# One encoder layer on one Trainium2 core: the FFN up product with seven block products in place of eight

## Chip, core and metric

The kernel runs on one core of one Trainium2 chip. The metric is the device time of one execution in microseconds (us). A profiled execution also leaves a trace: what each engine did (PE is the matrix engine, PEld its weight loads, DVE the vector engine, ACT the scalar engine, POOL the GpSimd engine, SP the engine whose queue issues nearly all transfers here), and what it waited for.

## The reference, cut to what matters

Two batches (`x_prompt`, `x_sample`) of 512 tokens and 1024 columns go through one layer with shared weights. The change is in the last part and at the passage into it:

```python
x = x + (g_a * a_out + g_b * b_out) @ w_o          # (512, 1024), each batch
xn2 = _rmsnorm(x, norm2_g)
up = xn2 @ w_up                                    # (1024) x (1024, 6144)
gate, val = jnp.split(up, 2, axis=-1)              # 3072 columns each
gate = _dwconv(gate, ffn_conv_w, ffn_conv_b)       # 3 taps over the tokens
x = x + (jax.nn.gelu(gate) * val) @ w_down         # (3072) x (3072, 1024)
```

## The kernel before

All data are 32-bit. Every matrix product is made of three matmuls: each operand is split into a rounded part `hi` and a remainder `lo`, and hi x hi, hi x lo and lo x hi are added up in a PSUM bank. A matmul has a 128 x 128 stationary operand and 512 moving columns.

The order of instructions on each engine is the order in which the program emits them; nothing reorders them. Weights come through one list of slabs (128 x 512), `specs`, in the order of use. `Stream.adv` splits the next slab: `hi` is an ACT copy (L225), `lo` a POOL subtraction (L226). `Stream.loads` issues the slabs' transfers on SP up to three ahead, and a ring of eight `hi`/`lo` pairs holds what PE has not used yet.

The stages at the end of the kernel:

- For each batch, `mix_tile` (8 times), then `o_phase`: 16 groups of 12 matmuls (L984 to L986) into `pso`, each added to the residual tile `acc[t]` (128 tokens x 1024) by DVE (L987). All eight `acc` tiles stay in SBUF to the end.
- After a tile's last group, `norm2_tile` squares and sums it on ACT (L286), makes the factor on POOL (L287, L288) and scales the tile into a copy `x2s` on POOL (L290). `norm2_T` transposes it on PE (L967) and splits it: DVE times the gain (L970), ACT `x2h` (L971), DVE `x2l` (L972).
- `up(f)`, for 24 column tiles f: gate and value columns, both batches, 8 depth blocks, 3 matmuls, into two-bank PSUM tiles; so 96 matmuls per f (L148 to L150). `gate_conv` and `h_out` make the convolution, the GELU, the product with the value half and its split `hh`, `hl`.
- `down(f)`, for pairs of f, stands between the `up` calls (`ffn_order`): 16 groups of 6 matmuls (L1090 to L1092), each added to `acc` by DVE (L1093).

Of the kernel before, what the change touches and what calls it, by code (L numbers as in the profile page):

```python
# [19 lines left out]
D = 1024  # L20
# [43 lines left out]
class Stream:  # L64
# [6 lines left out]
    def __init__(self, specs, load, split, cap, bufs):  # L71
        self.specs, self.load, self.split, self.cap, self.bufs = specs, load, split, cap, bufs
        self.raw, self.out = {}, {}
        self.nl = self.ns = self.nu = 0
        self.live = {}

    def loads(self):
        while self.nl < min(len(self.specs), self.ns + self.cap):
            self.raw[self.nl] = self.load(self.specs[self.nl])
            self.nl += 1  # L80

    def adv(self, n):

        self.loads()
        for _ in range(n):
            if self.ns == len(self.specs):
                return
# [25 lines left out]
def layer_kernel(ctx: ExitStack, tc: tile.TileContext, xs_in, norm1_g, w_in, conv_w, conv_b, lru_wa, lru_ba,  # L113
# [21 lines left out]
    o_d = dram.tile([S, 512], F32, name="o_d")  # L135

# [56 lines left out]
    def up_specs(f):  # L193
        return col_slabs(w_up, 128 * f, KD) + col_slabs(w_up, FF + 128 * f, KD)

    def down_specs(f):
        return [row_slab(w_down, f + j, 512 * h) for j in range(2) for h in range(2)]

    ffn_order = [("u", 0)]
    for f in range(1, NF - 3, 2):  # L200
        ffn_order += [("u", f), ("u", f + 1), ("d", f - 1)]
    ffn_order += [("u", NF - 3), ("u", NF - 2), ("u", NF - 1), ("d", NF - 4), ("d", NF - 2)]
    for t, f in ffn_order:
        specs += up_specs(f) if t == "u" else down_specs(f)
# [3 lines left out]
    def wload(spec):  # L208
        r = sa.tile([128, 512], F32, tag="raw", bufs=3, name="raw")
        _, src, nk = spec  # L210
        if nk:
# [5 lines left out]
    def wsplit(spec, r):  # L217
        ring, _, nk = spec
        n = 128 * nk if nk else 512
# [6 lines left out]
        lo_eng[0].tensor_tensor(out=lo[:, 0:n], in0=r[:, 0:n], in1=hi[:, 0:n], op=ALU.subtract)  # L226
        return hi, lo

    ws = Stream(specs, wload, wsplit, 3, {"a": 8, "b": 8})
    ws.open_ring("a")  # L230

# [575 lines left out]
    def combine(t, cg):  # L807
        d = p3.tile([128, 3, 8], F32, tag="cd", bufs=2, name="cd")
        e = p3.tile([128, 3, 8], F32, tag="ce", bufs=2, name="ce")
        m = p3.tile([128, 8], F32, tag="cm", bufs=2, name="cm")  # L810
# [96 lines left out]
    cm_acc0, acp0 = open_pool("acc0")  # L907
    cm_x20, x20p = open_pool("x2T0")
    cm_m, mp = open_pool("mix")
# [3 lines left out]
    def load_acc(b, pool):  # L913
        for i in range(4):
            acc[4 * b + i] = pool.tile([128, D], F32, name=f"acc{4 * b + i}")
            SP.dma_start(out=acc[4 * b + i], in_=xs_in[b][0, 128 * i:128 * i + 128, :])

    def new_x2(b, pool):
        x2[b] = (pool.tile([128, KD, S], F32R, name=f"x2h{b}"), pool.tile([128, KD, S], F32R, name=f"x2l{b}"))
# [11 lines left out]
    def mix_tile(b, c):  # L931
# [12 lines left out]
        mh = mp.tile([128, S], F32R, tag=f"mh{c}", bufs=1, name="mh")  # L944
        ml = mp.tile([128, S], F32R, tag=f"ml{c}", bufs=1, name="ml")
# [9 lines left out]
    def norm2_tile(t):  # L955
        x_t = mp.tile([128, D], F32, tag="x2s", bufs=3, name="x2s")
# [3 lines left out]
    def norm2_T(t):  # L960
        x_t = xst.pop(t)
        h, l = x2[t // 4]
        tl = slice(128 * (t % 4), 128 * (t % 4) + 128)
        for kk in range(0, KD, 4):
            pst = ps3.tile([128, 4, 128], F32, tag="t", bufs=4, name="pst")
# [27 lines left out]
    load_acc(0, acp0)  # L993
# [3 lines left out]
    new_x2(0, x20p)  # L997
# [3 lines left out]
    def hook0(n, i):  # L1001
# [168 lines left out]
```

## Time and profile before

| | |
|---|---|
| time, median of 3 runs | 2149.46 us (2149.22 to 2152.23) |
| profiled execution, its own time | 2149.69 us |
| its span in the trace | 2147.6 us |
| PE busy | 2087.7 us, 97% |
| PEld, DVE, ACT, POOL busy | 82%, 51%, 36%, 28% |
| mean granted TensorE clock | 0.99 of 2.4 GHz |
| data moved | 182 MB, mean 85 GB/s |

A matmul's shown duration overlaps the next one's, so PE's pace is read from the starts of matmuls that follow each other, and idle time from what stands between them. The time lies some 2 us above the span: what starts and ends the execution outside of the instructions.

### The profile page before, as it was taken

Reading aid. Unit: us, or ns where it says so; the run is one execution under the profiler, and the core shown is the slowest. Engines: PE = TensorE matmul, PEld = TensorE weight load, DVE = VectorE, ACT = ScalarE, POOL = GpSimd, SP = SyncE. Lnnn points to the kernel's source line nnn. Section 1 sums busy time; section 2 is a strip of 40 time slices with the busy share of each in tenths; the row PEclk is TensorE's granted clock in tenths of the full one; section 3 lists DMA queues with packets and bytes.
Section 4 is the critical chain, followed back from the end, with each engine's and each line's share of the span. In section 5 each row is a group of like instructions: output and inputs, shape, how many; then the busy total and the mean of one; then the engine's idle time right before and its main releaser. Section 6 shows DMA issues by size and latency. Waiting matters only on the chain. (4 is left out here: it accounts for less than half of the span.)

```text
span 2147.6 us, 25951 instructions
## 1 busy us (share of the span) xinstructions
PE 2087.7 (97%) x9859; PEld 1760.8 (82%) x9859; DVE 1084.7 (51%) x1581; ACT 783.5 (36%) x1321; POOL 601.7 (28%) x538
## 2 busy tenths in 40 slices
PE   7998898999999999999999999999999999999999
PEld 5876676887899999998777888888888888888887
DVE  5599998717862671675663442432233332333324
ACT  4388888622331242135433332422212122212120
POOL 3111111025113421413346455522222212221220
PEclk9999999999999999999999999999999999999999
DMA  4434354411111111103556445211111111111112
GB/s 143 150 104 133 106 141 130 146 50 40 36 41 46 40 54 54 36 16 119 186 180 193 145 151 174 65 38 57 49 49 47 52 40 50 49 51 47 54 45 84
DMA packets 190299, 181.98 MB, mean 85 GB/s; under 512 B 27708, under 2 KB 142942, under 8 KB 190174
## 3 DMA queue, kind: packets, MB, share of 16 engines
q1 hardware_dynamic: 188126, 175.08, 26.7%
q0 software_dynamic: 2048, 5.25, 1.0%
q8 instruction: 78, 1.28, 0.2%
q14 instruction: 47, 0.39, 0.1%
HBM read 141.80 MB, written 33.23 MB: 82 GB/s over the span
## 5 line engine op out<-in xcount | busy, mean ns | idle before, releaser
L226 POOL TENSOR_TENSOR lo<-raw,hi 128x512 fp32r<-128x512 f32 (+1 forms) x332 | 427.6, 1302 | 914.5 <-ACT hi L225 870.8
L225 ACT CAST hi<-raw 128x512 fp32r<-128x512 f32 (+1 forms) x376 | 219.6, 607 | 319.5 <-issue 117.9
L148 PE MATMUL ps<-x2h,hi 128*128 128x512 f32 x768 | 299.0, 389 | 0.0
L149 PE MATMUL ps<-x2l,hi 128*128 128x512 f32 x768 | 298.9, 389 | 0.0
L150 PE MATMUL ps<-x2h,lo 128*128 128x512 f32 x768 | 298.8, 389 | 0.0
L757 PE MATMUL ps<-hi,xh 128*128 128x512 f32 x576 | 251.4, 436 | 0.0
L758 PE MATMUL ps<-lo,xh 128*128 128x512 f32 x576 | 228.5, 397 | 0.0
L759 PE MATMUL ps<-hi,xl 128*128 128x512 f32 x576 | 228.3, 396 | 0.0
L1093 DVE TENSOR_TENSOR acc<-acc,psd 128x512 f32<-128x512 f32 x192 | 131.8, 687 | 190.8 <-PE psd L1092 190.8
L148 PE MATMUL ps<-xh,hi 128*128 128x512 f32 x544 | 219.4, 403 | 4.4 <-DVE xc L353 4.4
L150 PE MATMUL ps<-xh,lo 128*128 128x512 f32 x544 | 216.8, 399 | 0.0
L149 PE MATMUL ps<-xl,hi 128*128 128x512 f32 x544 | 216.8, 399 | 0.0
L149 PEld LDWEIGHTS ps<-x2l,hi 128*128 128x128 f32 x768 | 144.2, 188 | 30.1 <-DVE x2l L972 0.3
L148 PEld LDWEIGHTS ps<-x2h,hi 128*128 128x128 f32 x768 | 144.2, 188 | 29.8
L150 PEld LDWEIGHTS ps<-x2h,lo 128*128 128x128 f32 x768 | 144.2, 188 | 29.8
L757 PEld LDWEIGHTS ps<-hi,xh 128*128 128x128 f32 x576 | 156.1, 271 | 9.6
L758 PEld LDWEIGHTS ps<-lo,xh 128*128 128x128 f32 x576 | 158.3, 275 | 5.9
L759 PEld LDWEIGHTS ps<-hi,xl 128*128 128x128 f32 x576 | 156.4, 271 | 8.0
L1090 PE MATMUL psd<-hi,hh 128*128 128x512 f32 x384 | 149.4, 389 | 0.0
L1091 PE MATMUL psd<-lo,hh 128*128 128x512 f32 x384 | 149.4, 389 | 0.0
L1092 PE MATMUL psd<-hi,hl 128*128 128x512 f32 x384 | 149.4, 389 | 0.0
L1048 DVE SCALAR_TENSOR_TENSOR gc<-ps,vff,gc 128x1022 f32<-128x1022 f32 x24 | 30.8, 1282 | 225.3 <-ACT gc L1047 225.3
(188 smaller groups left out, 3467.0 us busy)
## 6 DMA issues: line engine op xcount, KB each, us to landing
raw<-in_w_in_dram SPq DMA_DIRECT2D x144, 256.0 KB
raw<-in_w_up_dram SPq DMA_DIRECT2D x96, 256.0 KB
raw<-in_w_down_dram SPq DMA_DIRECT2D x48, 256.0 KB
sg_d<-sgt SPq DMA_DIRECT2D x16, 512.0 KB
raw<-in_w_lru_out_dram SPq DMA_DIRECT2D x32, 256.0 KB
raw<-in_w_o_dram SPq DMA_DIRECT2D x32, 256.0 KB
cg<-num_d SPq DMA_DIRECT2D x24, 264.0 KB
num_d<-num SPq DMA_DIRECT2D x23, 264.0 KB
```

The lines of the kernel that those rows point to most:

```text
L148: PE.matmul(out=ps, lhsT=a, rhs=b, start=(k == 0), stop=False)
L149: PE.matmul(out=ps, lhsT=a, rhs=rl(k), start=False, stop=False)
L150: PE.matmul(out=ps, lhsT=wl(k), rhs=b, start=False, stop=(k == n - 1))
L225: A.copy(out=hi[:, 0:n], in_=r[:, 0:n])
L226: lo_eng[0].tensor_tensor(out=lo[:, 0:n], in0=r[:, 0:n], in1=hi[:, 0:n], op=ALU.subtract)
L757: PE.matmul(out=ps, lhsT=a, rhs=hi, start=(k == 0), stop=False)
L758: PE.matmul(out=ps, lhsT=a, rhs=lo, start=False, stop=False)
L759: PE.matmul(out=ps, lhsT=b, rhs=hi, start=False, stop=(k == KD - 1))
L1090: PE.matmul(out=ps, lhsT=a[0][:, tl], rhs=w[0], start=(i == 0), stop=False)
L1091: PE.matmul(out=ps, lhsT=a[0][:, tl], rhs=w[1], start=False, stop=False)
L1092: PE.matmul(out=ps, lhsT=a[1][:, tl], rhs=w[0], start=False, stop=(i == 1))
L1093: V.tensor_tensor(out=acc[t][:, cl], in0=acc[t][:, cl], in1=ps, op=ALU.add)
```

## The change

Take the up product's operands in 2 x 2 blocks: weights by column half (gate, value) and depth half, tokens by depth half and batch. Eight block products become seven, of 12 matmuls each (four depth blocks times three): per f 84 matmuls, not 96. With A11, A12 the two depth halves of a gate slab and A21, A22 those of the value slab, DVE makes the sums S1 to S4 of weights in SBUF before they are split. The sums of tokens are T1 to T4, with B11, B21 the depth halves of batch 0 and B22 the lower one of batch 1; each is kept as `hi` and `lo`. Products A11·B11, S2·T2, S3·T3 and A22·T4 add up in one bank (`pfA`), S1·T1 and S4·B22 in another (`pfC`), A12·B21 in a third (`pfB`); the partial sums wanted in between are copied out by ACT or added by DVE.

`acc` now holds one batch: each tile goes to DRAM (`acc_d`, L970) after its last `o_group`. For batch 1 `norm2_own` scales the tile in place, and `sums_T` transposes it and makes T1 to T4 and B22 (for a tile of 128 tokens: nine DVE, five ACT and four POOL instructions). For the first three f the two products without batch 1 (`batch0`) come first, between the transposes of tiles 0 to 3; the other five (`rest`) follow. Each f's result goes to DRAM (`f_d`), and the down product comes after all 24, with new `acc` tiles read back from `acc_d`.

```diff
+    def up_split(f, nm):
+        w = lambda key: upw[f, key]
+        add = lambda out, x, y, op: V.tensor_tensor(out=out, in0=x, in1=y, op=op)
+        if nm == ("S2" if f < EARLY else "A12"):
...
+            add(w("S1"), w("A21"), w("A22"), ALU.add)
+            add(w("S2"), w("S1"), w("A11"), ALU.subtract)
+        out = split_to("a", w(nm))
+        if nm == "S2":
+            add(w("A21"), w("A11"), w("A21"), ALU.subtract)
+            upw[f, "S3"] = w("A21")
+            add(w("A12"), w("A12"), w("S2"), ALU.subtract)
+            upw[f, "S4"] = w("A12")
...
+    def norm2_own(t):
+
+        store_acc(t)
+        junk = ps3.tile([128, D], F32, tag="m", bufs=2, name="junk")
...
+        act(out=junk, in_=acc[t], func=AF.Square, accum_out=ss)
+        G.tensor_scalar(out=ss, in0=ss, scalar1=1.0 / D, scalar2=EPS, op0=ALU.mult, op1=ALU.add)
+        G.tensor_tensor(out=rs, in0=ss, in1=mhalf[:, 0:1], op=ALU.pow)
+        V.tensor_scalar(out=acc[t], in0=acc[t], scalar1=rs, scalar2=None, op0=ALU.mult)
+
+    def sums_T(i, pst):
...
+        old = lambda nm, j: x2[nm][j][:, :, tl]
+        lo22 = put("B22", b22, G)
+        tt(V, t, b12, old("B11", 0), ALU.subtract)
+        tt(V, t, t, old("B11", 1), ALU.subtract)
+        lo22()
+        lo1 = put("T1", t, V)
+        tt(G, b12, b22, b12, ALU.subtract)
+        lo3 = put("T3", b12, G)
+        lo3()
+        tt(V, b22, b22, t, ALU.subtract)
+        lo1()
+        lo2 = put("T2", b22, V)
+        tt(V, t, old("B21", 0), b22, ALU.subtract)
+        lo2()
+        tt(V, t, t, old("B21", 1), ALU.add)
+        put("T4", t, G)()
...
+    lo_eng[:] = [V, G]
+    h0, h1 = ws.take(4), None
+    for n, (i, hlf) in enumerate(((0, 0), (1, 0), (0, 1), (1, 1), (2, 0), (2, 1), (3, 0), (3, 1))):
+        if n == 2:
+            h1 = ws.take(4)
+        o_group(4 + i, 1, hlf, h1 if hlf else h0, n >= 6)
+        if n < 6:
+            ws.adv(2)
+        if hlf:
+            norm2_own(4 + i)
+        if n in (5, 7):
+            sums_o((n - 5) // 2)
...
+    def prod(ps, slab, op, start, free=True):
...
+        for k in range(4):
+            a = wh[:, 128 * k:128 * k + 128]
+            kw = dict(skip_group_check=True)
+            PE.matmul(out=ps, lhsT=a, rhs=bh[:, k], start=(start and k == 0), stop=False, **kw)
+            PE.matmul(out=ps, lhsT=a, rhs=bl[:, k], start=False, stop=False, **kw)
+            PE.matmul(out=ps, lhsT=wl[:, 128 * k:128 * k + 128], rhs=bh[:, k], start=False, stop=(k == 3), **kw)
+        if free:
+            ws.done("a", 1)
+            ws.adv(1)
...
+    def batch0(f):
+
+        pa, pb = bank("A"), bank("B")
+        prod(pa, ws.take(1)[0], "B11", True)
+        p1[f] = row("p1", EARLY)
+        A.copy(out=p1[f], in_=pa)
+        prod(pb, ws.take(1)[0], "B21", True)
+        g0s[f] = row("g0", EARLY)
+        V.tensor_tensor(out=g0s[f], in0=p1[f], in1=pb, op=ALU.add)
+        return pa
+
+    def rest(f, pa):
...
+        prod(pa, ws.take(1)[0], "T2", early)
+        if early:
+            V.tensor_tensor(out=u2, in0=p1[f], in1=pa, op=ALU.add)
+        else:
+            A.copy(out=u2, in_=pa)
+        prod(pc, ws.take(1)[0], "T1", True)
+        if early:
+            V.tensor_tensor(out=p5, in0=p1[f], in1=pc, op=ALU.add)
+        else:
+            A.copy(out=p5, in_=pc)
+        prod(pa, ws.take(1)[0], "T3", False)
+        V.tensor_tensor(out=p5, in0=p5, in1=pa, op=ALU.add)
+        prod(pc, ws.take(1)[0], "B22", False)
+        V.tensor_tensor(out=g1, in0=u2, in1=pc, op=ALU.add)
...
+        prod(pa, ws.take(1)[0], "T4", False)
+        V.tensor_tensor(out=gc[:, 1], in0=gc[:, 1], in1=p5, op=ALU.mult)
+        if early:
+            V.tensor_tensor(out=p5, in0=p1[f], in1=pa, op=ALU.add)
+            V.tensor_tensor(out=gc[:, 0], in0=gc[:, 0], in1=p5, op=ALU.mult)
+        else:
+            V.tensor_tensor(out=gc[:, 0], in0=gc[:, 0], in1=pa, op=ALU.mult)
+        SP.dma_start(out=f_d[128 * f:128 * f + 128, :], in_=gc.rearrange("p b t -> p (b t)"))
...
+    batch0(0)
+    sums_f(2)
+    batch0(1)
+    sums_f(3)
+    batch0(2)
...
+    for f in range(NF):
...
+        pa = None if f < EARLY else batch0(f)
+        if f == NF - 1:
+            h_pair(0, (V, G))
+        rest(f, pa)
```

Where the instructions stand. In the rows below a name in brackets is what the instruction waits for; DMAHW is a transfer.

First place, DVE, the end of the output product of batch 1. Before, from the last additions of the third tile on:

```order
L987 TENSOR_TENSOR acc_11023<-acc_11023,pso 128x512 [waits DVE_49,PE_49]
L970 TENSOR_TENSOR x2g<-pst,v_71 128x512 [waits PE_49]
L972 TENSOR_TENSOR x2l_11015<-x2g,x2h_11014 128x4x128 [waits Activation_49]
L970 TENSOR_TENSOR x2g<-pst,v_71 128x512 [waits PE_49]
L972 TENSOR_TENSOR x2l_11015<-x2g,x2h_11014 128x4x128 [waits Activation_49]
L987 TENSOR_TENSOR acc_11025<-acc_11025,pso 128x512 [waits PE_49]
```

Of the change, from the last addition of tile 0 to the second operation of `sums_T` of tile 0:

```order
L1041 TENSOR_TENSOR acc<-acc,pso 128x512 [waits DVE_49,PE_49]
L1103 TENSOR_SCALAR acc<-acc,sr_75 128x1024 [waits DMAHW7_49,Activation_49,Pool_49]
L1041 TENSOR_TENSOR acc<-acc,pso 128x512 [waits PE_49]
L1103 TENSOR_SCALAR acc<-acc,sr_76 128x1024 [waits DMAHW0_49,Activation_49,Pool_49]
L1041 TENSOR_TENSOR acc<-acc,pso 128x512 [waits PE_49] x2
L1103 TENSOR_SCALAR acc<-acc,sr_75 128x1024 [waits DMAHW1_49,Activation_49,Pool_49]
L1116 TENSOR_TENSOR b_11342<-pst,v_73 128x512 [waits PE_49]
L1116 TENSOR_TENSOR b_11343<-pst,v_73 128x512
```

The scaling has moved from POOL (into a copy) to DVE (in place), where it waits for the transfer that stores the same tile, and the next tile's addition stands behind it. The nine DVE operations of a tile follow where four stood.

Second place, DVE, one f of the up product from the fourth on, up to its last operation. Of the change:

```order
L259 TENSOR_TENSOR s_12212<-r_12151,r_12153 128x512 [waits DMAHW7_49,DMAHW0_49,Pool_49]
L259 TENSOR_TENSOR s_12213<-s_12212,raw 128x512 [waits DMAHW5_49,DVE_49]
L259 TENSOR_TENSOR r_12151<-raw,r_12151 128x512 [waits Pool_49]
L259 TENSOR_TENSOR raw<-raw,s_12213 128x512 [waits DMAHW6_49,DVE_49,Pool_49]
L1212 TENSOR_TENSOR p_12198<-p_12198,pfA 128x512 [waits PE_49,Activation_49]
L1214 TENSOR_TENSOR g_12199<-u_12197,pfC 128x512 [waits PE_49]
L1219 SCALAR_TENSOR_TENSOR gc<-g_12194,vff,gc 128x511 [waits DMAHW1_49,Activation_49]
L1221 SCALAR_TENSOR_TENSOR gc<-g_12194,vff,gc 128x511 [waits DVE_49]
L1219 SCALAR_TENSOR_TENSOR gc<-g_12199,vff,gc 128x511 [waits Activation_49]
L1221 SCALAR_TENSOR_TENSOR gc<-g_12199,vff,gc 128x511 [waits DVE_49]
L1225 TENSOR_TENSOR gc<-gc,p_12198 128x512 [waits Activation_49]
L1230 TENSOR_TENSOR gc<-gc,pfA 128x512 [waits PE_49]
```

The four sums of the next f's weights (L259) stand ahead of the operations that empty this f's banks; with the addition of `pfB` (L1191) ahead of them an f has 13 DVE operations of 512 columns.

Third place, PE, where the up product ends and the down product begins. Of the change:

```order
L1173 MATMUL pfA<-T_11042,hi 128x512
L1174 MATMUL pfA<-T_11043,hi 128x512
L1175 MATMUL pfA<-T_11042,lo 128x512
L1287 MATMUL psd<-hi,hp 128x512 [waits DVE_49]
L1288 MATMUL psd<-lo,hp 128x512 [waits Pool_49]
L1289 MATMUL psd<-hi,hp 128x512
```

The first down matmul waits for DVE: it takes the bank that the last product (A22·T4 of f = 23) was added up in. Before, down products stood between up products, with banks of their own.

## Rows read from the trace of the kernel before

**Rows 1.** The page: span, and busy time of each engine with its share.

```profile
span 2147.6 us, 25951 instructions
PE 2087.7 (97%) x9859; PEld 1760.8 (82%) x9859; DVE 1084.7 (51%) x1581; ACT 783.5 (36%) x1321; POOL 601.7 (28%) x538
```

**Rows 2.** The page: shares of the span on the chain that ended last.

```profile
PE 44%; DMA 0%; SPq 0%; DVE 0%; issue 0%
```

**Rows 3.** Busy time by stretch: engines in order, granted clock, share and GB/s of DMA.

```profile
1235.00:1358.00 123.00, 123.00 (x560) 102.16 (x559) 44.74 (x64) 39.66 (x72) 65.34 (x59) 1.00 0.47 146
1358.00:2144.00 786.00, 785.96 (x3478) 650.67 (x3476) 257.84 (x303) 164.04 (x223) 189.90 (x146) 1.00 0.17 52
```

**Rows 4.** The same, over the passage from output product to up product.

```profile
1314.00:1374.00 60.00, 60.00 (x281) 49.78 (x280) 24.32 (x36) 20.57 (x36) 29.43 (x29) 1.00 0.34 110
```

**Rows 5.** Groups by line, 1358 to 2144 us: count, busy us, mean ns, idle before.

```profile
L148 PE MATMUL ps<-x2h,hi 128*128 128x512 f32 x768 | 299.0, 389 | 0.0
L226 POOL TENSOR_TENSOR lo<-raw,hi 128x512 fp32r<-128x512 f32 x141 | 186.3, 1341 | 560.2 <-ACT hi L225 560.2
L1090 PE MATMUL psd<-hi,hh 128*128 128x512 f32 x384 | 149.4, 389 | 0.0
L1093 DVE TENSOR_TENSOR acc<-acc,psd 128x512 f32<-128x512 f32 x192 | 131.8, 687 | 190.8 <-PE psd L1092 190.8
L225 ACT CAST hi<-raw 128x512 fp32r<-128x512 f32 x141 | 82.5, 616 | 188.1 <-issue 117.9 <-DMA raw<-in_w_up_dram 36.1 <-PE ps L149 17.2
L1062 DVE TENSOR_TENSOR hl<-gc,hh 128x1024 fp32r<-128x1024 f32 x24 | 29.6, 1233 | 18.4 <-ACT hh L1060 18.4
L1052 ACT ACTIVATE gc<-gc 128x1024 f32<-128x1024 f32 x24 | 25.5, 1062 | 62.7 <-DVE gc L1050 62.7
```

**Rows 6.** PE in order of time: two starts, 49 matmuls apart.

```profile
1490.99 0.39 PE L1090 MATMUL psd<-hi,hh 128*128 128x512 f32 x1
1502.10 0.39 PE L1091 MATMUL psd<-lo,hh 128*128 128x512 f32 x1
```

**Rows 7.** DVE in order of time, at the passage.

```profile
1351.40 0.69 DVE L987 TENSOR_TENSOR acc<-acc,pso 128x512 f32<-128x512 f32 x1 [2.04 <-PE pso L986]
1354.13 0.69 DVE L987 TENSOR_TENSOR acc<-acc,pso 128x512 f32<-128x512 f32 x1 [2.04 <-PE pso L986]
1356.60 1.29 DVE L972 TENSOR_TENSOR x2l<-x2g,x2h 128x512 fp32r<-128x512 f32 x1 [1.19 <-ACT x2h L971]
1360.28 0.68 DVE L987 TENSOR_TENSOR acc<-acc,pso 128x512 f32<-128x512 f32 x1
1360.87 0.68 DVE L970 TENSOR_TENSOR x2g<-pst,v 128x512 f32<-128x512 f32 x1
1362.74 0.69 DVE L972 TENSOR_TENSOR x2l<-x2g,x2h 128x512 fp32r<-128x512 f32 x1 [1.19 <-ACT x2h L971]
```

**Rows 8.** POOL there.

```profile
1356.06 1.29 POOL L226 TENSOR_TENSOR lo<-raw,hi 128x512 fp32r<-128x512 f32 x1
```

**Rows 9.** ACT there.

```profile
1364.07 0.62 ACT L971 CAST x2h<-x2g 128x512 fp32r<-128x512 f32 x1 [1.36 <-DVE x2g L970]
```

**Rows 10.** DVE, scaling a 128x1024 tile in place: shortest, median, longest ns.

```profile
L292 DVE TENSOR_SCALAR xt<-xt,sr x8: 752/754/754, 6.4 to 30.4; 128x1024 f32<-128x1024 f32 x8
```

**Rows 11.** SP: issue of four 512 KB loads.

```profile
1313.79 1.75 SPq L916 DMA_DIRECT2D acc<-in_x_sample_dram  x4
```

**Rows 12.** DVE, waiting for those loads.

```profile
1317.67 0.69 DVE L987 TENSOR_TENSOR acc<-acc,pso 128x512 f32<-128x512 f32 x1 [0.95 <-DMA acc<-in_x_sample_dram]
1320.53 0.69 DVE L987 TENSOR_TENSOR acc<-acc,pso 128x512 f32<-128x512 f32 x1 [2.17 <-DMA acc<-in_x_sample_dram]
```

**Rows 13.** SP: issue of a 256 KB load.

```profile
1189.11 0.43 SPq L1006 DMA_DIRECT2D yst<-y_d  x1
```

**Rows 14.** ACT, waiting for that load.

```profile
1191.88 0.62 ACT L796 CAST yh<-yst 128x512 fp32r<-128x512 f32 x1 [1.97 <-DMA yst<-y_d]
```

**Rows 15.** Busy time by stretch around a pause of PE.

```profile
44.00:50.00 6.00, 2.08 (x10) 1.38 (x8) 3.85 (x4) 1.20 (x1) 2.97 (x3) 0.93 0.58 169
50.00:55.00 5.00, 4.53 (x11) 3.59 (x12) 4.78 (x9) 0.41 (x2) 0.00 (x0) 0.50 0.55 116
55.00:60.00 5.00, 5.00 (x22) 4.06 (x21) 4.20 (x25) 0.85 (x2) 0.00 (x0) 0.90 0.59 224
```

More of the change, by code (lines that the diff above doesn't have):

```diff
@@ new lines, in layer_kernel @@
+    close(cm_mb, cm_ps)
+    cm_ps, ps4 = open_pool("ps4", space=PSUM)
+    cm_f, fp = open_pool("ffn")
+    up_pool[0] = fp
+    ws.limit = len(specs)
+    g0s, p1 = {}, {}
+    def prod(ps, slab, op, start, free=True):
+        wh, wl = slab
+        bh, bl = x2[op]
+        for k in range(4):
+            a = wh[:, 128 * k:128 * k + 128]
[3 more added lines that the diff above has]
+            PE.matmul(out=ps, lhsT=wl[:, 128 * k:128 * k + 128], rhs=bh[:, k], start=False, stop=(k == 3), **kw)
+        if free:
+            ws.done("a", 1)
+            ws.adv(1)
@@ new lines, in layer_kernel @@
+    bank = lambda nm: ps4.tile([128, 512], F32, tag=nm, bufs=2, name="pf" + nm)
+    row = lambda nm, bufs=1: fp.tile([128, S], F32, tag=nm, bufs=bufs, name=nm)
+    def batch0(f):
[7 more added lines that the diff above has]
+        return pa
@@ new lines, in sums_f, with h_fetch, h_pair @@
+    def sums_f(i):
+        sums_T(i, ps4.tile([128, 2, 512], F32, tag="t", bufs=1, name="pst"))
+    hraw, hT = {}, {}
+    def h_fetch(f):
+        t = acp.tile([128, T], F32, tag=f"acc{f % 4}", bufs=1, name="hraw")
+        SP.dma_start(out=t, in_=f_d[128 * f:128 * f + 128, :])
+        hraw[f] = t
+    def h_pair(f, engs):
+        nm = "B11" if f % 4 == 0 else "B21"
+        hh, hl = (x20p.tile([128, 2, T], F32R, name="hp", tag=nm + x, bufs=1) for x in "hl")
+        for j in range(2):
+            r = hraw.pop(f + j)
+            A.copy(out=hh[:, j], in_=r)
+            engs[j].tensor_tensor(out=hl[:, j], in0=r, in1=hh[:, j], op=ALU.subtract)
+        hT[f] = (hh, hl)
@@ new lines, in layer_kernel @@
+    batch0(0)
[3 more added lines that the diff above has]
+    batch0(2)
+    close(cm_st)
+    lo_eng[:] = [G]
+    for f in range(NF):
+        if f == NF - 1:
+            for j in range(4):
+                h_fetch(j)
+        pa = None if f < EARLY else batch0(f)
+        if f == NF - 1:
+            h_pair(0, (V, G))
+        rest(f, pa)
+    close(cm_f, cm_b, cm_ps)
+    cm_ps, ps5 = open_pool("ps5", space=PSUM)
+    cm_d, dp = open_pool("accd")
+    for t in range(8):
+        acc[t] = dp.tile([128, D], F32, name=f"accd{t}")
+        SP.dma_start(out=acc[t], in_=acc_d[128 * t:128 * t + 128, :])
@@ L1081, in down @@
+    for f in range(0, NF, 2):
         w4 = ws.take(4)
-        tiles = [hT.pop(f), hT.pop(f + 1)]
+        hh, hl = hT.pop(f)
         for t in range(8):
```

267 lines of the change are left out of this document (135 added, 132 removed).

## The prediction

> **What bounds the kernel now.** I read the page first: PE is busy 97% of the span [rows 1], and PE's own work is nearly all of the part of the chain of waits that the page follows [rows 2]. Then the stretches: over the up and down products, 1358 to 2144 us, PE is busy 785.96 of 786.00 us, DVE, ACT and POOL 258, 164 and 190, at full granted clock, with DMA at 17% [rows 3]; over the passage into the stage it is 60.00 of 60.00 us [rows 4]. So in the stage that the change touches only fewer matmuls, or new waits of PE, can change the time. A matmul's shown 389 ns [rows 5] overlap the next one's. The pace comes from two starts 49 matmuls apart in a down product: (1502.10 - 1490.99) / 49 = 0.2267 us [rows 6]. It holds for the whole stage: three lines of 768 and three of 384 matmuls [rows 5] are 3456, times 0.2267 = 783.5 us of the 786. A group of 12 takes 2.72 us, which is also the distance of two additions of the output product (1354.13 - 1351.40) [rows 7]. What the change disturbs in the passage now costs nothing.
>
> **What the change removes.** Per f 84 matmuls for 96, so 24 x 12 = 288 fewer: 288 x 0.2267 = 65.3 us. Down, output and transpose matmuls keep their numbers.
>
> **A cycle of the up product, f from 3 on.** PE needs 7 x 2.72 = 19.05 us. DVE has 13 operations of 512 columns; such an operation takes 0.69 us, from PSUM [rows 5] or from SBUF [rows 7], so 8.97 us. POOL has seven `lo` at 1.34 [rows 5], 9.4 us. ACT has seven `hi` and three bank copies of 0.62, two of 512 columns for the convolution at about the same, and a GELU of 1.06 [rows 5], 8.5 us. One thing makes that less loose. A DVE subtraction with both inputs in SBUF took 1.29 us when it began (1356.60) while POOL was in a `lo` (1356.06, 1.29 long), and 0.69 at other times [rows 7, 8]; additions from PSUM show no such growth. But even if DVE and POOL took turns in everything, 8.97 + 9.4 = 18.4 us, below 19.05. Following the order in a cycle, PE's waits are met: T3's product waits for a copy made right after T2's, with T1's 2.72 us between; T4's waits for the addition after T3's, with B22's between. The GELU chain ends about 2.9 us after T4's product, but the next f has the other `pfA` bank. A slab is split six products ahead of its use. The SP queue gives 4 loads and a store per f; the store waits for DVE's last product, and the next load behind it is needed much later. All in all 32 MB more go out and back through DRAM, and DMA stands at 17%. Cost: 0. If that cover were gone, every microsecond per cycle would cost 21.
>
> The Trainium skill, page "SBUF — State Buffer", section "SBUF: two separate sides", says that DVE with two SBUF inputs and a GpSimd operation that reads SBUF hold a shared port exclusively, for a whole instruction. The 1.29 us agree with it. By it the nine such operations of a cycle and POOL's seven take turns: 9 x 0.69 + 9.4 = 15.6 us, and the sum stays; a version of it in which both sides lose is the second rival.
>
> **The passage into the up product, the dear part.** Before, POOL scaled a copy and DVE had four short operations per tile. Now DVE's queue is a chain; PE does nothing there that DVE doesn't wait for or hold up. I follow it from the end of the group that completes tile 0 (time 0). Prices: DVE 512 columns 0.61 in a row (1360.28 to 1360.87) and 0.69 alone [rows 7]; POOL 1.29 [rows 8]; ACT copy 0.62 [rows 9]; scaling a tile 0.75 [rows 10]. No row shows a 512 KB store that somebody waits for. The nearest row, a load of that size, was issued at 1313.79 and let DVE begin at 1317.67, 3.9 us [rows 11, 12]; a 256 KB load took 2.8 [rows 13, 14]. I take 3.9, with 2.8 as the lower bound and 6.7 (to the second load's addition at 1320.53) as the upper.
>
> - Tile 0's addition ends at 0.7. The scaling in place waits for the store: 0.7 + 3.9 + 0.75 = 5.35. Tile 1's addition stands behind it: 6.0, store and scaling to 10.65. Then the two additions of the next groups and tile 2's store and scaling: 16.55.
> - `sums_T` of a tile: two products 1.2, ACT 0.6, POOL 1.29, POOL 1.26 (DVE's next operation waits for both), DVE 0.65, one that meets POOL 1.25, three more 1.87: 8.1 us. Tile 0: 24.65.
> - Then `lo` of the early slabs: ACT's last copy and the slab's (1.2), POOL's `lo` until 1.9, so the first ends at 27.15. The fifth slab's load waits on SP for that, lands 2.8 later and is copied by ACT: its `lo` ends at 31.2. Tile 3's addition stands behind it: 31.9; store and scaling: 36.55.
> - Tile 1's sums: 44.65. S1 and S2 (one behind POOL) 2.5, copy and `lo` of S2 1.2, S3, S4 and the addition of `pfB` 1.9: 50.2. Tile 2's sums: 58.3, a `lo` and an addition behind POOL 3.1: 61.4. Tile 3 to T2's `lo`: 7.5.
> - So the first product with T2 can begin at 68.9 us. PE's work till then is 5 groups of 2.72, 32 transposes at 0.11 (some 3.5) and 6 products of 2.72: 33.4. PE stands for 35.5 us. It must stand, since the `batch0` products take banks that tile 1's sums and the last square (behind the slabs on ACT) must first be done with.
>
> The bounds of this: DVE's operations in that time add up to some 34 us without waits, so at best about 1 us; with 6.7 us per store and more meetings with POOL about 50. I take 35.5, since the waits are in the order and not chosen by the chip.
>
> The Trainium skill, page "DMA: Bandwidth & Descriptors", section "Anatomy of one DMA", puts a transfer at about 2.0 us plus bytes / 436e3. By it a 512 KB store would take 3.2 us, and with four of them the sum would be 2.8 us lower; the 3.9 of the load is what a row shows.
>
> **The first three `rest`.** They have five products of PE (13.6 us) for 15 DVE operations, and T3's product waits for a DVE addition (`u2`) instead of an ACT copy. Behind T2's `lo` DVE still has the rest of tile 3, a `lo`, four weight sums and an addition: `u2` ends at 77.0, where PE is ready at 74.35: 2.7. In the second and third `rest`, `u2` stands behind five operations of the convolution chain, four sums and three products: 1.5 and 1.1. Together 5.3 us, bounds 0 (DVE catches up) and 10.
>
> PE's clock: where PE was busy for only 2.08 of 6 us, the granted clock was 0.50, the 1.2 GHz level, in the next 5 us, and 0.90 in the 5 after [rows 15]. The same may come behind the last stand, and would make T2's product 2.7 us longer. That lies inside the 2.7 us in which T3's would wait for `u2`, so it adds 0; without that cover 2.7.
>
> **From up to down.** The last T4 product's bank is the first that the down product takes. After B22's product come an addition 0.69, four operations at 0.65, the GELU 1.06 and two products 1.3: 5.65 us, less T4's 2.72: PE stands for 2.9 us. (Bounds: 0, if the bank were another; 5, if POOL is in the way.) Then the eight `acc` loads are issued; the first lands about 4 us later, the others at distances of up to 2.9 [rows 12], while seven further banks let PE run 1.36 us each and the eighth tile is wanted 20 us later. The split of the first `h` pair stands beside f = 23: cost 0.
>
> **Sum**, against the profiled execution's 2149.69 us, which agrees with the median 2149.46: 2149.69 - 65.3 + 35.5 + 5.3 + 2.9 = 2128.1.
>
> **Rivals.**
> 1. The passage is hidden. For it: DVE's plain work fits PE's. Against: three waits for stores stand in one in-order queue. Time: with 1 us of stand, nothing in the `rest`, 1 at the end, 2086; with half of 35.5, about 2110. Chance of less than 2103: 0.10.
> 2. Slower: the up cycle is set by DVE and POOL in turn, where both lose: nine DVE operations at 1.29 and four at 0.69 are 14.4, POOL 9.4, together 23.8 us for 19.05; 21 cycles make 2128 + 100 = 2228. It decides from a cycle of 20.1 us (21.6 us of gain over 21 cycles). Against it: six products of lead, and 258 of 786 us of DVE now, where each `lo` keeps 1.34 us. Chance 0.09.
> 3. The passage and the first `rest` at their upper bounds: 2149.69 - 65.3 + 50 + 10 + 5 = 2149.4, no change. Chance of 2143 to 2154: 0.07.
> That the saved matmuls don't come off has almost no room: PE's pace is the same 0.227 us in all products.
>
> **Chances.** The forecast, 2103 to 2143, holds 0.74. A measurement of this kernel tells about 0.2% (4.3 us) from no change: faster is below 2145.2, slower above 2153.8. Faster: 0.74 + 0.10 = 0.84; same 0.07; slower 0.09. The range takes some of rivals 1 and 3: 2100 to 2150.
>
> **What would show it.** After: 2016 up matmuls at 0.227 us and a repeat of f in 19.05 us, PE gapless from f = 3 to 23 (else rival 2). PE idle about 35 us between the end of tile 0's last group and the first product with T2, in pieces before tile 1's transposes, the first `batch0`, tile 3's transposes and T2; DVE idle for DMA some 3 us before each L1103 (none: rival 1). A clock dip there. One stand of about 3 us before the first down matmul. The prediction fails if DVE's L1103 doesn't wait for stores, or if a cycle is longer than 20 us.

## The result, and the profile after

| | before | after |
|---|---|---|
| time, median | 2150.28 us (2149.22 to 2152.23, 4 runs) | 2130.43 us (2129.79 to 2132.91, 4 runs) |
| ratio to before | | 0.9909 (95% interval 0.9892 to 0.9926) |
| profiled execution, its time and span | 2149.69, 2147.6 us | 2130.6, 2128.8 us |
| matmuls | 9859 | 9571 |
| data moved | 182 MB | 217 MB |

The changed kernel is faster by 19.9 us, 0.9%. The page of after has the lines that answer to [rows 1, 2]:

```profile
span 2128.8 us, 26423 instructions
PE 2030.3 (95%) x9571; PEld 1710.2 (80%) x9571; DVE 1253.8 (59%) x1850; ACT 870.4 (41%) x1495; POOL 741.7 (35%) x626
PE 76%; DVE 12%; ACT 5%; issue 3%; DMA 2%; POOL 1%; SPq 0%; DVEq 0%; ACTq 0%; POOLq 0%
```

288 matmuls are gone, 65.3 us at 0.2267, but the span fell by 18.8 only. The part of the chain that ended last was PE's alone as far as the page followed it before (44% of the span, [rows 2]); now it has DVE, ACT and DMA in it. Two of the stretches of [rows 3, 4] now look like this (same columns), with the up product from 1420 and the down product from 1860 apart:

```profile
1358.00:1420.00 62.00, 34.92 (x127) 27.70 (x128) 42.21 (x55) 22.57 (x39) 36.03 (x26) 0.71 0.22 64
1420.00:1860.00 440.00, 434.49 (x1907) 358.38 (x1905) 231.02 (x307) 182.01 (x294) 218.16 (x159) 1.00 0.29 89
1860.00:2125.00 265.00, 262.65 (x1152) 217.17 (x1152) 148.85 (x204) 47.28 (x66) 80.71 (x54) 0.99 0.32 111
```

In the passage PE is busy 34.92 of 62 us, at a mean granted clock of 0.71; in the two products behind it PE is nearly gapless again. PE's waits from 1300 us on (what waited, on what: us in total, times, longest), of which the kernel before had none in this part:

```profile
PE pfA L1173 <- ACT junk L1100: 15.2, 1, 15.2
PE pfA L1173 <- ACT T L1121: 8.3, 1, 8.3
PE pst L1110 <- DVE b L1116: 5.5, 2, 5.3
PE psd L1287 <- DVE gc L1230: 3.4, 1, 3.4
PE pfA L1173 <- ACT hi L227: 2.2, 1, 2.2
PE pfA L1174 <- DVE T L1117: 1.4, 1, 1.4
PE pfA L1173 <- ACT u L1205: 1.1, 1, 1.1
PE pfA L1173 <- DVE u L1203: 1.1, 1, 1.1
```

Below, PE in order of time, at the start of batch 1's output product, at the first products with T2, and where the down product begins:

```profile
1308.98 0.39 PE L1035 MATMUL pso<-hi,mh 128*128 128x512 f32 x1
...
1406.31 0.80 PE L1173 MATMUL pfA<-T,hi 128*128 128x512 f32 x1 [8.32 <-ACT T L1121]
1408.54 0.79 PE L1174 MATMUL pfA<-T,hi 128*128 128x512 f32 x1 [1.43 <-DVE T L1117]
...
1409.55 0.63 PE L1173 MATMUL pfA<-T,hi 128*128 128x512 f32 x1
1409.98 0.63 PE L1174 MATMUL pfA<-T,hi 128*128 128x512 f32 x1
...
1447.64 0.47 PE L1173 MATMUL pfA<-T,hi 128*128 128x512 f32 x1 [2.22 <-ACT hi L227]
...
1862.35 0.79 PE L1287 MATMUL psd<-hi,hp 128*128 128x512 f32 x1 [3.43 <-DVE gc L1230]
```

From 1308.98 to the second T2 matmul, the first one that needs T2's `lo`, are 99.6 us. PE's work in it is 192 matmuls of the output product and 73 of up (60.1 us) and 32 transposes (3.5), so 36.0 us are lost there: 30.4 us in which PE stands, and 5.6 us from matmuls at half the pace. Behind it starts are 0.43 us apart (1409.55 to 1409.98), half the pace.

And DVE in order of time, the chain that sets this:

```profile
1339.17 0.69 DVE L1041 TENSOR_TENSOR acc<-acc,pso 128x512 f32<-128x512 f32 x1 [1.50 <-PE pso L1037]
1342.59 0.75 DVE L1103 TENSOR_SCALAR acc<-acc,sr 128x1024 f32<-128x1024 f32 x1 [2.73 <-DMA acc_d<-acc]
...
1352.38 1.28 DVE L1116 TENSOR_TENSOR b<-pst,v 128x512 f32<-128x512 f32 x2
...
1357.36 0.69 DVE L1117 TENSOR_TENSOR b<-b,t 128x512 f32<-128x512 f32 x1 [2.38 <-POOL b L1117]
...
1358.69 1.63 DVE L1117 TENSOR_TENSOR t<-B,b 128x512 f32<-128x512 f32 x1
...
1371.96 0.75 DVE L1103 TENSOR_SCALAR acc<-acc,sr 128x1024 f32<-128x1024 f32 x1 [3.21 <-DMA acc_d<-acc]
1372.63 1.28 DVE L1116 TENSOR_TENSOR b<-pst,v 128x512 f32<-128x512 f32 x2
```

Tile 0's sums begin 13.2 us after its last addition (1352.38 - 1339.17), with three waits for a store between (2.73, 2.75 and 3.08); the fourth stands right ahead of tile 1's sums.

The store is only the last of two things that a scaling waits for. The other is its factor, which ACT's square (L1100) and two POOL operations make; of tile 0 it is there 0.6 us before the store:

```profile
1341.41 0.55 POOL L1102 TENSOR_TENSOR sr<-sr,mhalf 128x1 f32<-128x1 f32 x1
```

From the end of the addition to the end of this operation are 2.1 us (1339.86 to 1341.96), and 2.1, 2.2 and 2.5 us for the other tiles. So by these rows DVE would have stood about 8.8 of the 11.8 us with no store at all. No run here takes out the store alone.

### The profile page after: what moved, and what is told of

It reads as the page before. It is cut to its first block, busy times and chain, and to the rows that moved or that the text cites. A ratio compares the mean times of both kernels' runs of the same rounds, so it can differ in the third digit from the quotient of the medians.

```text
span 2128.8 us, 26423 instructions
## 1 busy us (share of the span) xinstructions
PE 2030.3 (95%) x9571; PEld 1710.2 (80%) x9571; DVE 1253.8 (59%) x1850; ACT 870.4 (41%) x1495; POOL 741.7 (35%) x626
## 4 chain that ended last, share of the span: by engine, by line
PE 76%; DVE 12%; ACT 5%; issue 3%; DMA 2%; POOL 1%; SPq 0%; DVEq 0%; ACTq 0%; POOLq 0%
PE ps L807 7%; PE ps L808 6%; PE ps L809 6%; PE ps L151 5%; PE ps L152 5%; PE ps L153 5%; PE psd L1287 4%; PE psd L1289 4%; PE psd L1288 4%; PE pfA L1174 4%; PE pfA L1173 4%; PE pfA L1175 4%; DVE u L486 3%; PE o L728 3%; PE pfC L1174 2%
## 5 line engine op out<-in xcount | busy, mean ns | idle before, releaser
L230 POOL TENSOR_TENSOR lo<-raw,hi 128x512 fp32r<-128x512 f32 (+1 forms) x303 | 394.2, 1315 | 643.2 <-ACT hi L227 607.9
L1290 DVE TENSOR_TENSOR accd<-accd,psd 128x512 f32<-128x512 f32 x192 | 130.9, 686 | 115.3 <-PE psd L1289 109.7
L1287 PE MATMUL psd<-hi,hp 128*128 128x512 f32 x384 | 150.1, 391 | 3.4 <-DVE gc L1230 3.4
L1289 PE MATMUL psd<-hi,hp 128*128 128x512 f32 x384 | 149.9, 390 | 0.0
L1288 PE MATMUL psd<-lo,hp 128*128 128x512 f32 x384 | 149.9, 390 | 0.0
L707 ACT ACTIVATE p<-p,nm 128x128 f32<-128x128 f32 (+1 forms) x192 | 81.7, 427 | 146.2 <-DVE nm L705 146.2
L629 DVE TENSOR_REDUCE ss<-sq 128x8 f32<-128x512 f32 x48 | 32.9, 685 | 163.6 <-ACT sq L626 163.6
L1173 PE MATMUL pfA<-T,hi 128*128 128x512 f32 x288 | 113.9, 396 | 12.7 <-ACT T L1121 8.3
L151 PEld LDWEIGHTS ps<-xh,hi 128*128 128x128 f32 x544 | 105.2, 193 | 24.6 <-issue 1.4
L152 PEld LDWEIGHTS ps<-xl,hi 128*128 128x128 f32 x544 | 105.1, 193 | 22.2
L153 PEld LDWEIGHTS ps<-xh,lo 128*128 128x128 f32 x544 | 104.7, 192 | 22.7
L1174 PE MATMUL pfA<-T,hi 128*128 128x512 f32 x288 | 113.8, 395 | 1.4 <-DVE T L1117 1.4
```

Of the source, the lines that this page charges most:

```text
L151: PE.matmul(out=ps, lhsT=a, rhs=b, start=(k == 0), stop=False)
L152: PE.matmul(out=ps, lhsT=a, rhs=rl(k), start=False, stop=False)
L153: PE.matmul(out=ps, lhsT=wl(k), rhs=b, start=False, stop=(k == n - 1))
L230: e.tensor_tensor(out=lo[:, 0:n], in0=r[:, 0:n], in1=hi[:, 0:n], op=ALU.subtract)
L1174: PE.matmul(out=ps, lhsT=a, rhs=bl[:, k], start=False, stop=False, **kw)
L1287: PE.matmul(out=ps, lhsT=hh[:, i, tl], rhs=w[0], start=(i == 0), stop=False)
```

## The experiments

The theory was: DVE's in-order chain of four waits ahead of the scalings and four tiles' sums sets the start of T2; a bank sets the start of down; the up cycle hides DVE and POOL. The rivals: POOL, PE or the transfers set the passage; other things hold down; DVE and POOL in turn set the cycle. All kernels but e4 are edits of the changed kernel. In the table, "passage" runs from the first `pso` matmul of batch 1's output product to the first T2 matmul, "up" from there to the last up matmul, "to down" from that to the first `psd` matmul (0.23 is no wait).

| kernel | median us | ratio to before (95%) | passage | up | to down |
|---|---|---|---|---|---|
| after | 2130.43 | 0.9909 (0.9892 to 0.9926) | 97.3 | 452.2 | 3.82 |
| e1 scalings later | 2126.18 | 0.989 (0.9875 to 0.9905) | 91.9 | 451.8 | 3.80 |
| e2 `lo` of B22 on DVE | 2129.86 | 0.9905 (0.989 to 0.992) | 95.3 | 451.2 | 3.82 |
| e3 an unused tile (no change) | 2130.84 | 0.9911 (0.9896 to 0.9926) | 97.3 | 451.3 | 3.81 |
| e4 before, four slab buffers | 2143.86 | 0.9975 (0.9965 to 0.9984) | | | |
| e5 `lo` twice | 2164.18 | 1.007 (1.0055 to 1.0085) | 97.4 | 486.6 | 3.82 |
| e6 other banks | 2124.96 | 0.9891 (0.9874 to 0.9907) | 97.5 | 450.1 | 0.23 |
| e7 sums earlier | 2129.96 | 0.9908 (0.9893 to 0.9922) | 96.7 | 450.1 | 3.82 |
| e8 e7 + e2 + e6 | 2125.43 | 0.9887 (0.9873 to 0.9902) | 94.4 | 452.1 | 0.22 |
| e9 e1 + e2 + e6 | 2119.76 | 0.9869 (0.9853 to 0.9886) | 89.0 | 449.6 | 0.23 |
| e10 after again | 2129.59 | 0.9913 (0.9898 to 0.9927) | 97.3 | 451.8 | 3.81 |

The stretches ahead of the passage vary by some us from one execution to the next (in the traces of the changed kernel and its edits the passage begins between 1305.7 and 1311.0 us), so the edits are judged by their own stretch first. The passage itself is 97.3 to 97.5 us in all five traces that leave its order alone; the up stage, e5 aside, varies from 449.6 to 452.2 us with no clear tie to an edit.

**e1: the scalings later.** `norm2_own` hands back the scaling, which stands behind a later group:

```diff
-        V.tensor_scalar(out=acc[t], in0=acc[t], scalar1=rs, scalar2=None, op0=ALU.mult)
+        return lambda: V.tensor_scalar(out=acc[t], in0=acc[t], scalar1=rs, scalar2=None, op0=ALU.mult)
...
-            norm2_own(4 + i)
+            scale[i] = norm2_own(4 + i)
+        if n in (4, 5):
+            scale[n - 4]()
         if n in (5, 7):
             sums_o((n - 5) // 2)
+            scale[(n - 1) // 2]()
```

> The four in-place scalings of batch 1 are moved back in DVE's queue, behind the next tile's additions or behind a tile's sums, so that the store of the tile has landed when DVE comes to them; the work is the same. Theory (the stand is DVE's in-order chain, with four waits of 2.7 to 3.2 us for stores in it): 11 us leave the chain, the first product with T2 comes about 56 us after the end of the group that completes tile 0 instead of 67.2, and the span is about 2118 us. Rival (PE is held by the bank that the last square writes and by the slabs behind the sums on ACT, whatever DVE waits for): less than 2 us, 2127 or more.

The passage fell by 5.4 us, half of what the theory said and more than the rival's 2. DVE of e1, in order of time:

```profile
1340.11 0.69 DVE L1041 TENSOR_TENSOR acc<-acc,pso 128x512 f32<-128x512 f32 x1 [1.52 <-PE pso L1037]
1342.83 0.69 DVE L1041 TENSOR_TENSOR acc<-acc,pso 128x512 f32<-128x512 f32 x1 [2.03 <-PE pso L1037]
...
1346.15 0.75 DVE L1103 TENSOR_SCALAR acc<-acc,sr 128x1024 f32<-128x1024 f32 x1
...
1348.88 0.75 DVE L1103 TENSOR_SCALAR acc<-acc,sr 128x1024 f32<-128x1024 f32 x1
1349.54 1.28 DVE L1116 TENSOR_TENSOR b<-pst,v 128x512 f32<-128x512 f32 x2
...
1365.96 1.28 DVE L1116 TENSOR_TENSOR b<-pst,v 128x512 f32<-128x512 f32 x2
```

No L1103 waits for a store or a factor now, so e1 doesn't tell the two apart. But now DVE waits for PE's groups, 2.72 us each, and tile 0's sums, which stand behind the sixth group, begin 9.4 us after its last addition instead of 13.2. So of the first three waits (8.6 us) 3.8 us came back; tile 1's sums are 7.6 us earlier (25.9 us after that addition for 33.5). About 2 us are lost again behind them, where tile 3's scaling and DVE operations that meet POOL's now stand. The waits ahead of the scalings were in the chain, but removing a wait of the chain is worth only the distance to what comes next, here PE.

**e2: the `lo` of B22 on DVE**, with POOL's own subtraction (for T3) ahead of it:

```diff
-        lo22 = put("B22", b22, G)
+        lo22 = put("B22", b22, V)
...
+        tt(G, b12, b22, b12, ALU.subtract)
         lo22()
         lo1 = put("T1", t, V)
-        tt(G, b12, b22, b12, ALU.subtract)
```

> In each tile's sums the remainder of B22 is made by DVE instead of POOL. Theory (DVE waits about 2.4 us per tile for two POOL operations in a row; one of them goes): about 1.7 us per tile, 7 us in all, span about 2122 us. Rival (DVE's own work is the bound, and it gets 0.69 us more per tile): 3 us longer, about 2132.

2.0 us in the passage, 0.5 per tile, between the theory (7) and the rival (3 us longer); the median doesn't show it (2129.86 for 2130.43 and 2129.59 of the unchanged kernel). DVE of e2, at the place of the 1357.36 row above:

```profile
1355.43 1.76 DVE L1117 TENSOR_TENSOR B<-b,B 128x512 fp32r<-128x512 f32 x1
1357.30 0.69 DVE L1117 TENSOR_TENSOR b<-b,t 128x512 f32<-128x512 f32 x1
1357.91 1.75 DVE L1117 TENSOR_TENSOR T<-t,T 128x512 fp32r<-128x512 f32 x1
```

The wait of 2.38 for POOL is gone, but the moved `lo` takes 1.76 us beside POOL's work instead of 0.69, and T1's `lo` 1.75 for 0.68, while T4's first subtraction, 1.63 in the changed kernel, is back at 0.69: most of the wait moved into DVE operations that meet POOL's.

**e3 and e6: whose bank holds down.** e3 takes out one unused tile ahead of the down product's first; e6 deals out the up stage's PSUM tags anew:

```diff
-        pa, pb = bank("A"), bank("B")
+        pa, pb = bank("C" if f < EARLY else "A"), bank("B")
...
+        pc = bank("C")
         if early:
             pa = bank("A")
-        pc = bank("C")
```

> The down product begins with the second of the eight banks, so that the bank of the last up product comes eighth. Theory (the stand between up and down is the wait for that bank, and the slow matmuls behind it follow from the stand): the 3.6 us and 1.3 us of half clock go, span about 2124 us. Rival (PE then waits for the additions, which wait for the residual tiles read back from DRAM; the first was there 8.8 us after the last up matmul, seven banks cover 9.5): a stand of some us appears a few groups later, and the span stays above 2127.

> The PSUM tags of the up stage are dealt out anew so that the bank that the down product's first group takes is the one that the last B22 product used, whose reader is done at 1857, and the bank of the last T4 product is needed by no group of down before the eighth. Theory A (the 3.4 us wait of the first down group is for the bank that the last gate multiplication reads): the wait goes, the half clock after it as well, and the time falls by 3.4 to 4.9 us, to 2125.5 to 2127. Rival (it is something that any bank would wait for, such as the operands of down or the closing of the pool): the wait stays on the first down matmul and the time is within 1 us of 2130.4.

In e3 the wait stayed as it was, 3.4 us at the first down matmul. The tile that nothing writes is not in the program at all: e3 is the changed kernel, instruction for instruction, and so neither of its theories was tried. It is one more measurement of that kernel. In e6, PE in order of time:

```profile
1855.63 0.39 PE L1287 MATMUL psd<-hi,hp 128*128 128x512 f32 x1
...
1856.76 0.39 PE L1289 MATMUL psd<-hi,hp 128*128 128x512 f32 x1
1859.22 0.50 PE L1287 MATMUL psd<-hi,hp 128*128 128x512 f32 x1 [2.07 <-DVE gc L1230]
1859.56 0.40 PE L1288 MATMUL psd<-lo,hp 128*128 128x512 f32 x1
```

The first group's six matmuls (1855.63 to 1856.76) now follow the last up matmul without a wait; the wait moved to the second group and shrank to 2.07 us, and no half pace follows. So it was the bank that the last gate product reads; the wait is for one bank, not for the stage. It is met at the second group and not at the eighth, as the expectation had it, because the program's down groups take the banks in the order 0, 7, 6 and on down to 1; the last T4 product has bank 0 in the changed kernel and bank 7 in e6. From the last up matmul to the last of down it is now 263.5 us, for 266.1 in the changed kernel: 2.6 us. The rest of the 5.5 us between the medians isn't accounted for by this edit: in the traces 1.2 us lie ahead of the passage and 2.1 us in the up stage, which varies as much without it.

**e4: the kernel before with four buffers** for weight slabs in flight instead of three, as the changed kernel has them; small tiles have one buffer less to make room.

```diff
-        r = sa.tile([128, 512], F32, tag="raw", bufs=3, name="raw")
+        r = sa.tile([128, 512], F32, tag="raw", bufs=4, name="raw")
...
-        x_t = mp.tile([128, D], F32, tag="x2s", bufs=3, name="x2s")
+        x_t = mp.tile([128, D], F32, tag="x2s", bufs=2, name="x2s")
```

> The kernel before with nothing of the change but its numbers of buffers: four raw slab buffers instead of three, and fewer of the small combine tiles and of the scaled copies. Theory (the changed kernel's lead of 6 to 7 us at 85 us, of which 4 are left at 1309 us, comes from the fourth raw slab being loaded earlier at the start): about 4 us less, 2143 to 2146, with DVE's wait of 4.0 us for a slab at 46 us gone. Rival (the lead comes from something else in the changed program, or from the run): 2148 to 2150.

5.4 us by the ratio (0.9975), as the theory said, without any block product. In the kernel before, DVE and the output product of batch 1 begin like this:

```profile
46.08 0.43 DVE L223 CAST hi<-raw 128x512 fp32r<-128x512 f32 x1 [4.01 <-DMA raw<-in_w_in_dram]
...
1313.12 0.39 PE L984 MATMUL pso<-hi,mh 128*128 128x512 f32 x1
```

In e4 the fourth slab is there at once, the same cast in one go with three others:

```profile
40.67 1.42 DVE L223 CAST hi<-raw 128x512 fp32r<-128x512 f32 x4
```

And two of the stretches of [rows 15] in e4:

```profile
44.00:50.00 6.00, 5.71 (x25) 4.43 (x24) 4.76 (x5) 1.21 (x1) 2.99 (x3) 1.00 0.65 178
50.00:55.00 5.00, 5.00 (x24) 4.14 (x23) 4.37 (x20) 1.26 (x3) 0.00 (x0) 1.00 0.59 182
```

So the pause of PE and the half clock behind it are gone. e4's output product of batch 1 begins 5.6 us earlier than before (1307.56). The changed kernel has the same buffers, and the cast of four slabs in one go as well; it starts the passage 4.1 us earlier (1308.98 for 1313.12).

**e5: more work for POOL in the up cycle.** From f = 3 on, five of the seven slabs have their `lo` subtracted twice; the numbers are the same.

```diff
         out = split_to("a", w(nm))
+        if f >= EARLY and nm not in ("A22", "S4"):
+            G.tensor_tensor(out=out[1], in0=w(nm), in1=out[0], op=ALU.subtract)
```

> From the fourth up column on, GpSimd repeats the subtraction that makes the low part of five of the seven weight slabs (the same numbers are written twice, so the output is unchanged). GpSimd's work in an up cycle goes from 7 to 12 of its 1.29 us subtractions, 15.5 us, and VectorE keeps its 12 operations, of which the four sums of slabs, the four convolution operations and the first gate multiplication read nothing but SBUF, 6.2 us unhindered. Theory A of the prediction (the two engines take turns only where both work on SBUF, and the cycle of 19.05 us had room for 9 + 6.2 us): the sum is now 21.7 us, 2.6 us more than TensorE's 19.05, so 21 cycles are about 55 us longer, 2185 in all, with TensorE waiting for weight slabs in each of them. Rival (the two do not hinder each other enough to add up, each has its own 19.05 us): 15.5 us still fits, time within 5 us of 2130. If the rival's time comes, the cover of the up cycle was larger than the prediction made it.

34.4 us in the up stage: from the second on, the cycles are 20.5 to 20.7 us long for 19.04. That lies between the two theories. In e5, groups of DVE by line, 1634 to 1824 us (count, busy us, mean ns, idle before):

```profile
L1223 DVE SCALAR_TENSOR_TENSOR gc<-g,vff,gc 128x511 f32<-128x511 f32 x18 | 29.9, 1661 | 0.6
L1221 DVE SCALAR_TENSOR_TENSOR gc<-g,vff,gc 128x511 f32<-128x511 f32 x18 | 24.5, 1364 | 0.0
...
L1214 DVE TENSOR_TENSOR p<-p,pfA 128x512 f32<-128x512 f32 x10 | 6.7, 674 | 0.0
```

and PE's waits:

```profile
PE pfA L1175 <- ACT p L1190: 24.8, 20, 1.3
```

with ACT in one cycle, in order of time:

```profile
1646.57 1.06 ACT L1225 ACTIVATE gc<-gc 128x1024 f32<-128x1024 f32 x1 [5.22 <-DVE gc L1223]
...
1648.56 0.58 ACT L1190 COPY p<-pfA 128x512 f32<-128x512 f32 x1
```

The convolution's operations, 0.75 us in the changed kernel, take 1.36 and 1.66; those that read PSUM stay at 0.67. But PE doesn't wait for a weight slab, as expected; it waits for the copy of the first product (`p`). That copy stands on ACT behind the GELU (1646.57), and the GELU had waited for the slower convolution (L1223). So the cover of the up cycle ends in this chain, before DVE and POOL in turn fill a cycle: POOL still stands idle 2.3 us per cycle (20.6 us in nine, waiting for ACT's `hi`). In the changed kernel the cover holds.

**e7 and e8: the sums earlier.** As e1, with the scalings of the first three tiles behind the fourth, fifth and seventh group and the sums of tiles 0 and 1 one group earlier:

```diff
+        if n in (3, 4, 6):
+            scale[{3: 0, 4: 1, 6: 2}[n]]()
+        if n in (4, 6):
+            sums_o((n - 4) // 2)
+        if n == 7:
+            scale[3]()
```

> As in the kernel with the scalings later, but the sums of the first two tiles also move up by one output group each (after the fifth and the seventh group of eight instead of the sixth and the eighth), and each scaling stands at least one group behind its store. Theory A (after the scalings were moved, the sums could not start before TensorE's next group was through, so only 3.8 us of the first three store waits came back): the sums start one group, 2.7 us, earlier than there and the passage falls by about as much, time 2122 to 2125. Rival (the chain behind the sums, the weight slabs' own low parts and POOL, sets the first T2 product): the passage stays at 48 us within 1 us and the time at 2126.

> The early sums of the kernel above, the low part of B22 by VectorE, and the other PSUM banks together. If the gains add up: 2.7 to 8 us from the passage, 2 us from B22 and 3.4 to 4.9 us from the banks, so 2117 to 2123. If the passage is held by another engine once the waits are gone, the first two overlap and the time is 2121 to 2126.

Neither of e7's theories came: against e1, e7 is slower, and the passage is 96.7 us. DVE of e7:

```profile
1370.41 0.67 DVE L1041 TENSOR_TENSOR acc<-acc,pso 128x512 f32<-128x512 f32 x1
1374.29 0.75 DVE L1103 TENSOR_SCALAR acc<-acc,sr 128x1024 f32<-128x1024 f32 x1 [3.21 <-DMA acc_d<-acc]
1378.04 0.69 DVE L259 TENSOR_TENSOR s<-r,r 128x512 f32<-128x512 f32 x1 [2.99 <-DMA r<-in_w_up_dram]
```

and SP's issues:

```profile
1371.12 0.34 SPq L970 DMA_DIRECT2D acc_d<-acc  x1
...
1372.92 1.19 SPq L245 DMA_DIRECT2D r<-in_w_up_dram  x2
```

The sums of tile 1 now stand ahead of tile 3's last addition, which ends at 1371.1 although its passage began 4.2 us earlier than e1's, where it ends at 1366.0. Tile 3's store waits for it, the loads of the first up slabs stand behind that store on SP, and DVE waits for them (2.99) and for the store (3.21). What was gained at tile 0 was given back through SP's queue. e8, with the two other edits, carries this loss too and comes out where the second of its forecasts has it.

**e9 and e10: what gained alone, together**, and the changed kernel beside it on the same chip.

> The three edits that each gained alone, without the early sums: scalings later (the passage from the start of the second output phase to the first T2 product fell from 97.3 to 91.9 us), the low part of B22 by VectorE (95.3 us) and the other PSUM banks (last up product to first down product 3.8 to 0.2 us, and no half clock behind it). If the first two add up, the passage is 90 us, and the time is 2119 to 2123. If the second is hidden once the first is in, the passage is 91.5 to 92 and the time 2121 to 2124.5. If the result is 2125 or above, as with the early sums, some stage other than these three has lost what they gain.

> The changed kernel itself once more, on the same chip as the kernel above, so that the two stand beside each other: 2128 to 2132 by its four runs so far, and 0.990 to 0.992 of the kernel before.

The first two edits add up, as the first of the forecasts has it: e9's passage is 89.0 us, 8.3 less than after, a little more than the two apart (5.4 and 2.0). Its time is 9.8 us below e10's and 1.3% below the kernel before, the fastest of these kernels. The two longest of PE's waits in the passage that are still there:

```profile
PE pfC L1177 <- ACT junk L1100: 11.4, 1, 11.4
PE pfA L1177 <- ACT T L1121: 8.0, 1, 8.0
```

## Why the prediction was right, and where its terms were not

2128 was predicted and 2130.43 measured. The steps, from the rows above and the starts in the trace of after:

| term | predicted us | measured us |
|---|---|---|
| 288 matmuls fewer | -65.3 | -65.3 |
| stages ahead of the passage | 0 | -4.1 |
| passage, to T2's `lo` | +35.5 | +36.0 |
| first three `rest` | +5.3 | +8.4 |
| up cycles | 0 | 0 to f = 22, +1.4 at f = 23 |
| from up to down | +2.9 | +5.0 |
| sum | -21.6 | -18.6 (spans: -18.8) |

That the forecast lies within 3 us is in part luck: 7.1 us of terms that were priced too low or at nothing stand against 4.1 us of gain ahead of the passage that the prediction didn't have.

- **Removed matmuls.** Right. PE's pace is the same, and no wait of PE stands between 1447.64 and 1850.46.
- **The passage.** The mechanism was right: DVE's order, with PE standing at three of the four places named (before the first `batch0` 15.2 us, before tile 3's transposes 5.3, before T2 8.3, half pace behind each); before tile 1's transposes it stood only 0.2. T2's `lo` came 69.4 us after the end of tile 0's group for 68.9 predicted. Two errors cancelled: the scaling stood 2.7 to 3.2 us behind the addition, not 3.9, some 3.8 us less over four; and a tile's sums took 9.15 us (1352.38 to 1361.53), not 8.1, some 4.2 more, since POOL's results came 2.4 us late and DVE operations that met POOL took 1.63 to 1.75, not 1.25. The prediction put the whole wait down to the store. The store does end it, but the square and the factor, which have no term in the prediction, end only 0.6 to 0.9 us sooner. The Trainium skill, page "DMA: Bandwidth & Descriptors", section "Anatomy of one DMA", has the sum that gave 3.2 us for such a store as an estimate, for transfers issued by GpSimd; these stores went out from SP, and DVE began 2.7 to 3.2 us after their issue, nearer to that estimate than to the load that the prediction used. e1 and e2 show that both parts, the waits ahead of the scalings and POOL in the sums, are in the chain, and that neither is worth its full length when removed.
- **The first three `rest`.** Mis-sized. The clock dip came as foreseen: 2.9 us of half pace behind T2, and with it no wait for the first `u2`. The second waited 1.3 us for 1.5. The third `rest` waited not for `u2` (1.1) but for the `hi` of a weight slab, whose sum (L259) was late on DVE: 2.4 us, and half pace behind it, 1.7.
- **The up cycle.** Right with cost 0. At f = 23 the split of the first `h` pair was not free: its ACT copies (L1250) waited for their loads, and the `u` copy behind them on ACT came 1.1 us late.
- **From up to down.** The place and the bank were right (e6). DVE's four convolution operations took 3.1 us to the GELU's start (1856.84 to 1859.91), not 2.6, and B22's addition began 0.2 us after the product's last start was through, so PE stood 3.6 us; and the half pace behind it, 1.4 us, was not priced there.
- **Ahead of the passage.** The step that the prediction left out. The change also raises the slab buffers from three to four, which the diff shown with the change leaves out, and the prediction has no term for it. It took only the clock from the pause of PE in the first stage [rows 15], the same pause in which DVE waited for a slab. e4 shows -5.4 us for the buffers alone, so some 4 to 5 of the measured 19.9 us, a fifth to a quarter, aren't from the block products.
- **Rivals.** That the passage is hidden is out: 36 us are there. The up cycle as the bound is out for this kernel, and e5 shows that it comes with five more POOL operations per cycle, by another chain than the one given.

## What to carry to other kernels

Fewer matmuls at the full pace of the engine save exactly their number times the pace; what decides is the passage where the new operands are made, and there one follows the in-order queue of the engine that makes them, with its waits for stores and for other engines' results, step by step. Where an instruction waits for two things, price both: here the later one, the store, came only 0.6 to 0.9 us behind the factor. Before taking a wait out, look at what ends next after it: half of the waits ahead of the scalings were worth nothing, mostly because PE's groups came next, and moving the sums still earlier only delayed a store and the loads behind it. A count of buffers that is changed for one stage changes all stages that use the pool: read the waits of the others too.

## What the runs showed of the hardware that was not expected

- A pause of PE of only 2.2 us (before 1447.64) was followed by starts 0.43 us apart from about 1449 to 1452, with a granted clock of 0.50, the 1.2 GHz level. The pause of 3.4 us before the down product was followed by this level at once (0.50 from 1862 to 1865), and so was the one of 4.4 us in the first stage of before [rows 15]. A pause of 2.07 us in e6 was not followed by it (1.00 from 1859 to 1862).
- DVE subtractions and convolution operations on SBUF beside POOL's subtractions took up to 1.78 us for 0.68, more than the 1.29 of [rows 7], and POOL's own took 1.62 to 1.75 for 1.29 in such places, while DVE operations that read PSUM kept 0.67 to 0.69 (e5). The ends show that the two took turns, with the wait inside the shown duration: the DVE operation ended 0.54 to 0.55 us after POOL's in before (1357.89 after 1357.35), in the changed kernel (1360.32 after 1359.78) and in e2 (1357.19 after 1356.64).
